# Projection stage of a hybrid streaming trunk: transposes traced one group later, two raw weight buffers, history copies on ScalarE

## The chip, the cores and the metric

The kernel runs on one core of one Trainium2 chip. The metric is the time of one execution on the device in microseconds (us). Of several timed executions the median is taken; a profile describes one further execution, with a time of its own. In the profile PE is TensorE (PEld is its weight load), DVE is VectorE, ACT is ScalarE, POOL is GpSimd, and SP is SyncE, whose queue issues nearly all DMAs.

## The reference

One layer of a streaming encoder with 2048 prompt tokens and 8 x 16 sample tokens, model width 1024, all in float32. Cut to what matters:

```
h = rmsnorm(x, norm1_g) * (1 + sc1) + sh1
proj = h @ w_in                              # 1024 -> q,k,v,gate | beta,a | q,k,v of group B
qkv  = silu(causal depthwise conv, width 4, of proj[q,k,v])     # group A: gated DeltaNet
q, k = l2norm(q) * DK**-0.5, l2norm(k)
o_a  = rmsnorm(chunked delta rule(q, k, v, beta, g)) * silu(gate)
qb, kb = rmsnorm(proj[qB]), rmsnorm(proj[kB])                   # group B: band attention
o_b  = softmax(qb @ kb^T * DH**-0.5 + bias over 9 chunks of 64) @ vb
x = x + gate1 * (concat(o_a, o_b) @ w_out)
x = x + gate2 * (relu(rmsnorm(x) * (1 + sc2) + sh2) @ w_up) ** 2 @ w_down
```

The states are outputs too: the last three rows ahead of the convolution, the delta-rule state, and the last keys and values of group B.

## The kernel before

**Precision and weights.** Each matrix product is made of three passes with operands split into a high and a low part (`hi` x `hi`, `hi` x `lo`, `lo` x `hi`). A weight tile of 512 KB comes to the chip in `weights` (lines 166 to 185): SP loads it into a `raw` buffer (L174, `bufs=self.nraw`), ACT casts it into the high half of a `w` buffer (L175, four buffers), and the low half is either a subtraction on POOL (L82, reading `raw` and the high half), or, once it has been stored, a second load from DRAM (L178). Which one it is depends on the block: `w_in` is subtracted and stored (L183) in the first block of phase 1 and loaded after that; `w_out`, `w_up` and `w_down` are subtracted in block 0 of phase 2, subtracted and stored in block 1, and loaded from block 2 on. So a `raw` buffer is free after the cast, or, where POOL subtracts, after the subtraction. It serves both phases: `run` sets `nraw` once.

**Phase 1** goes over six blocks of two or three tiles of 128 tokens. `proj_a` makes group A's projections: for each of four heads a group of 24 matmuls each for k, q and v (`psq`, L519 to L521, one weight tile, 384 columns), then on the way out of PSUM: two history copies of three columns (L527 before, L529 after), the copy to `pre` (L528, ACT), the convolution (one ACT operation, three DVE operations with `y`), tanh (ACT), and the last product into `kq` or `vT` (DVE). A step registered with `later` runs when `tick` has been called as often as its lag says; `tick` comes once for each group. That step, `qkv_out`, transposes the result on PE (`ptq`, L554), and copies or squares it. `proj_b` makes group B's projections; its keys go through `k_out`, which transposes them (`ptk`, L1011). The delta rule of the block before (lane 0 and 1 of the generators) is put between these groups as filling.

**Phase 2** goes over five blocks of two, four, four, four and three tiles: `out_proj`, then `ffn` with 64 weight tiles per block (32 of `w_up`, 32 of `w_down`); block 0 has two tiles, hence 256 columns per matmul of `w_up` and the shortest time for a weight tile. The attention of the next block's tiles fills in (L1250 to L1292).

**Order.** The Python order sets priorities; a scheduler then fixes each engine's order at build time by its own estimates, so an edit in one place moves rows on every engine. On the chip each engine takes its rows strictly in that order, SP's queue too.

Of the kernel before, what the change touches and what calls it, by code (L numbers as in the profile page):

```python
# [8 lines left out]
F32 = mybir.dt.float32  # L9
F32R = mybir.dt.float32r  # L10
# [4 lines left out]
P = 128  # L15
# [9 lines left out]
DH = 64  # L25
# [16 lines left out]
def bcast(ap, axis, n):  # L42
    dims = [list(x) for x in ap.ap]
    dims.insert(axis, [0, n])
    return bass.AP(tensor=ap.tensor, offset=ap.offset, ap=dims)
# [6 lines left out]
class Trunk:  # L52
# [415 lines left out]
    def proj_a(self, tiles, hT, nxt=()):  # L468

        nc = self.nc  # L470
        n = len(tiles)
        T = n * P
        smp = SMP in tiles
        Tp = T - (P if smp else 0)
        blk = {}
        blk["kq"] = []
        ssq = self.bp.tile([P, self.nt, AH], F32, tag="ssq", name="ssq", bufs=2)
        ssk = self.bp.tile([P, self.nt, AH], F32, tag="ssk", name="ssk", bufs=2)
        ba = self.bp.tile([P, self.nt, 8], F32, tag="ba", name="ba", bufs=2)

        def gates(half):

            xs = [] if half else [self.normed(None, t) for t in nxt]
            m = 256 + 8 * half
            ws = self.wslices("w_in", 0, GA0 + 256 * half, m, KT, 4)
            for j, tl in enumerate(tiles):
                tmps = self.load_a(nxt[j], xs[j], 0, 1) if j < len(xs) else None
                ps = self.gp.tile([P, 512], F32, tag="g", name="psg")
                for k in range(KT):
                    wh, wl = ws[k]  # L490
                    self.mm3(ps[:, 0:m], hT[:, k, 0, j * P:(j + 1) * P], hT[:, k, 1, j * P:(j + 1) * P], wh, wl,
                             k == 0, k == KT - 1)
                th = self.cp.tile([P, 256], F32, tag="th", name="th", bufs=1)
                sg = self.cp.tile([P, 256], F32, tag="sgw", name="sgw", bufs=2)
                self.act(th, ps[:, 0:256], AF.Tanh, scale=0.5)
                self.stt(sg, th, 1.0, ps[:, 0:256], ALU.add, ALU.mult)
                if half:
                    nc.scalar.copy(ba[:, j], ps[:, 256:264])
                sv = sg.rearrange("p (h d) -> p h d", d=P)
                self.tt(sv, sv, bcast(self.gdng, 1, 2), ALU.mult, eng=nc.gpsimd)  # L500
                nc.sync.dma_start(self.s_sg[tl][:, half * 256:(half + 1) * 256], sg)
                self.tick(24 * 256)
                if tmps:
                    self.load_b(j, tmps)
            for j in range(len(tiles), len(xs)):
                self.load_b(j, self.load_a(nxt[j], xs[j], 0, 1))

        gates(1)
        for h in range(AH):
            kq = self.bp.tile([P, 2, self.nt * P], F32, tag="kq", name="kq", bufs=8)  # L510
            blk["kq"].append(kq)
            for sec in (1, 0, 2):
                c = sec * 4 + h
                ws = self.wslices("w_in", 0, c * P, P, KT, KT)
                ps = self.gp.tile([P, 512], F32, tag="g", name="psq")
                for k in range(KT):
                    wh, wl = ws[k]
                    mm = nc.tensor.matmul
                    mm(ps[:, 0:T], wh, hT[:, k, 0, 0:T], start=(k == 0), stop=False)  # L519
                    mm(ps[:, 0:T], wh, hT[:, k, 1, 0:T], start=False, stop=False)  # L520
                    mm(ps[:, 0:T], wl, hT[:, k, 0, 0:T], start=False, stop=(k == KT - 1))  # L521
                self.tick(24 * T)
                pre = self.cp.tile([P, 3 + self.nt * P], F32, tag="pre", name="pre", bufs=2)
                dst = kq[:, 1 - sec] if sec < 2 else self.cp.tile([P, self.nt * P], F32, tag="vT", name="vT", bufs=2)
                y = self.cp.tile([P, self.nt * P], F32, tag="y", name="y", bufs=2)
                if Tp:
                    nc.vector.tensor_copy(pre[:, 0:3], self.hist[:, c])  # L527
                    nc.scalar.copy(pre[:, 3:3 + Tp], ps[:, 0:Tp])  # L528
                    nc.vector.tensor_copy(self.hist[:, c], pre[:, Tp:Tp + 3])  # L529
                    self.conv(y[:, 0:Tp], pre, c, Tp)  # L530
                if smp:
                    pres = self.cp.tile([P, NB, 3 + SL], F32, tag="pres", name="pres", bufs=2)
                    nc.vector.tensor_copy(pres[:, :, 0:3], self.hists[:, c].rearrange("p (b w) -> p b w", w=3))
                    nc.scalar.copy(pres[:, :, 3:], ps[:, Tp:T].rearrange("p (b s) -> p b s", s=SL))
                    nc.vector.tensor_copy(self.hists[:, c].rearrange("p (b w) -> p b w", w=3), pres[:, :, SL:SL + 3])
                    self.conv(y[:, Tp:T].rearrange("p (b s) -> p b s", s=SL), pres, c, P, sub=True)
                th = self.cp.tile([P, self.nt * P], F32, tag="cth", name="cth", bufs=2)
                self.act(th[:, 0:T], y[:, 0:T], AF.Tanh)
                self.stt(dst[:, 0:T], th[:, 0:T], 1.0, y[:, 0:T], ALU.add, ALU.mult)
                self.later(lambda c=c, dst=dst: self.qkv_out(c, dst, tiles, ssq, ssk))  # L540
                if self.bi:
                    self.mod_step()
        self.flush()
        gates(0)
        blk.update(ssq=ssq, ssk=ssk, ba=ba)
        return blk
# [417 lines left out]
    def proj_b_tile(self, sec, half, tl, hT, j, ws):  # L964
        nc = self.nc
        H = BH // 2
        cs = slice(half * 256, (half + 1) * 256)
        hs = slice(half * H, (half + 1) * H)
        ps = self.gp.tile([P, 512], F32, tag="g", name="psb")[:, 0:256]
# [25 lines left out]
        if tl >= 12:  # L995
            nc.sync.dma_start(
                self.o[nm + "band_prompt"][0, 0, (tl - 12) * P:(tl - 11) * P].rearrange("s h d -> s (h d)")[:, cs], raw)
        st = self.qp.tile([P, H, 2, DH], F32R, tag="stk", name="stk", bufs=3)
        self.split(st[:, :, 0], st[:, :, 1], rv)
        if sec == 2:  # L1000
            nc.sync.dma_start(self.s_kv[hs, :, tl, 1].rearrange("h p d -> p h d"), st.bitcast(F32).rearrange("p h a d -> p h (a d)"))
            return
        self.later(lambda: self.k_out(st, hs, tl), 2)

    def k_out(self, st, hs, tl):
        nc = self.nc
# [541 lines left out]
                self.ffn(tiles, self.hT, x1)  # L1548

    def run(self):  # L1550
        self.nraw, self.nw = 3, 4
        self.deferred, self.lanes, self.pending, self.fill_rate, self.fill_acc = [], ([], [], []), [0, 0, 0], 0.0, 0.0
        self.front, self.solved, self.spent = 0, 0, 0
        self.constants()
        self.phase1()
        self.phase2()
# [35 lines left out]
```

## Time and profile before

| what | value |
|---|---|
| median of 3 runs | 3242.33 us (3240.86 to 3249.45) |
| profiled execution, own time | 3235.24 us |
| its span, first to last instruction | 3233.5 us |
| TensorE clock granted, mean | 0.977 |
| PE busy | 3071.4 us, 95% |
| DVE, ACT, POOL busy | 59%, 46%, 22% |
| HBM traffic over the span | 226 GB/s |

Busy shares are means over stages with different limits, and matmul ends are modelled. So the table says that PE is the engine to follow, and that about 160 us of the span are left in which it stands still; where they lie is a question for the view of stretches.

### The profile page before, as it was taken

Reading aid. Unit: us, or ns where it says so; the run is one execution under the profiler, and the core shown is the slowest. Engines: PE = TensorE matmul, PEld = TensorE weight load, DVE = VectorE, ACT = ScalarE, POOL = GpSimd, SP = SyncE. Lnnn points to the kernel's source line nnn. Section 1 sums busy time; section 2 is a strip of 40 time slices with the busy share of each in tenths; the row PEclk is TensorE's granted clock in tenths of the full one; section 3 lists DMA queues with packets and bytes.
Section 4 is the critical chain, followed back from the end, with each engine's and each line's share of the span. In section 5 each row is a group of like instructions: output and inputs, shape, how many; then the busy total and the mean of one; then the engine's idle time right before and its main releaser. Section 6 shows DMA issues by size and latency. Waiting matters only on the chain.

```text
span 3233.5 us, 53068 instructions
## 1 busy us (share of the span) xinstructions
PE 3071.4 (95%) x19577; PEld 2713.0 (84%) x19577; DVE 1903.2 (59%) x4526; ACT 1478.5 (46%) x2707; POOL 701.2 (22%) x561
## 2 busy tenths in 40 slices
PE   7899999999999979988999999999999999998998
PEld 6798988899989968878888889888888887787997
DVE  5985777777868676888446567235455443243223
ACT  3554544556656555554424444344434443333332
POOL 4641312121222347653343320000000000000000
PEclk9999999999989999998999999999999999998999
DMA  9789896878888765565565666665676667677875
GB/s 298 225 264 283 269 288 207 266 236 245 282 292 262 223 201 167 160 222 174 170 200 188 204 214 228 195 195 186 204 246 191 209 230 230 222 239 224 258 246 195
DMA packets 624507, 730.71 MB, mean 226 GB/s; under 512 B 59040, under 2 KB 483088, under 8 KB 622200
## 3 DMA queue, kind: packets, MB, share of 16 engines
q1 hardware_dynamic: 618488, 695.87, 68.0%
q0 software_dynamic: 5760, 31.46, 3.0%
q8 instruction: 154, 2.52, 0.3%
q14 instruction: 105, 0.86, 0.1%
HBM read 614.57 MB, written 115.52 MB: 226 GB/s over the span
## 4 chain that ended last, share of the span: by engine, by line
PE 71%; DVE 12%; DMA 9%; issue 3%; ACT 2%; SPq 1%; POOL 1%; POOLq 0%; DVEq 0%; ACTq 0%
PE psd L164 7%; PE psd L162 7%; PE psu L1480 7%; PE psu L1481 7%; PE psd L163 7%; PE psu L1482 7%; PE pv L1285 2%; PE psq L521 2%; PE psq L520 2%; PE psq L519 2%; PE psb L162 2%; PE psb L164 2%; PE psb L163 2%; PE psS L1267 2%; PE pso L162 2%
## 5 line engine op out<-in xcount | busy, mean ns | idle before, releaser
L175 ACT CAST w<-raw 128x1024 fp32r<-128x1024 f32 (+1 forms) x528 | 552.7, 1048 | 349.2 <-PE psd L164 163.2
L82 POOL TENSOR_TENSOR w<-raw,w 128x1024 fp32r<-128x1024 f32 (+1 forms) x172 | 418.3, 2443 | 365.8 <-ACT w L175 327.5
L1480 PE MATMUL psu<-hT,w 128*128 128x512 f32 (+2 forms) x1304 | 468.6, 361 | 7.1 <-ACT hT L104 6.2
L1481 PE MATMUL psu<-hT,w 128*128 128x512 f32 (+2 forms) x1304 | 467.2, 359 | 1.2 <-DVE hT L82 1.2
L1482 PE MATMUL psu<-hT,w 128*128 128x512 f32 (+2 forms) x1304 | 465.7, 357 | 0.0
L164 PE MATMUL psd<-w,u 128*128 128x512 f32 x1088 | 431.4, 398 | 9.1 <-DVE u L82 9.1
L162 PE MATMUL psd<-w,u 128*128 128x512 f32 x1088 | 432.5, 398 | 7.9 <-DVE y L82 4.1
L163 PE MATMUL psd<-w,u 128*128 128x512 f32 x1088 | 427.6, 393 | 0.0
L82 DVE TENSOR_TENSOR r<-r 128x512 f32<-128x512 f32 (+2 forms) x160 | 178.8, 1117 | 399.7 <-ACT u L92 399.4
L82 DVE TENSOR_TENSOR y<-y,psd 128x512 f32<-128x512 f32 x238 | 162.2, 684 | 242.0 <-PE psd L164 241.4
L1480 PEld LDWEIGHTS psu<-hT,w 128*128 128x128 f32 x1304 | 246.6, 190 | 39.8 <-ACT hT L104 7.4
L1481 PEld LDWEIGHTS psu<-hT,w 128*128 128x128 f32 x1304 | 246.8, 189 | 33.2 <-DVE hT L82 2.3
L1482 PEld LDWEIGHTS psu<-hT,w 128*128 128x128 f32 x1304 | 246.6, 189 | 32.5 <-issue 0.2
L92 ACT ACTIVATE r<-psu 128x512 f32<-128x512 f32 (+2 forms) x160 | 85.5, 534 | 408.7 <-PE psu L1482 349.6
L164 PEld LDWEIGHTS psd<-w,u 128*128 128x128 f32 x1088 | 204.9, 189 | 56.7 <-DVE u L82 10.4
L162 PEld LDWEIGHTS psd<-w,u 128*128 128x128 f32 x1088 | 205.3, 189 | 53.5 <-DVE y L82 6.7
L163 PEld LDWEIGHTS psd<-w,u 128*128 128x128 f32 x1088 | 205.6, 189 | 45.4 <-issue 1.0
L162 PE MATMUL psb<-w,hT 128*128 128x256 f32 x816 | 236.3, 290 | 0.7 <-ACT qraw L976 0.7
L164 PE MATMUL psb<-w,hT 128*128 128x256 f32 x816 | 234.1, 288 | 0.5 <-DVE hT L82 0.5
L163 PE MATMUL psb<-w,hT 128*128 128x256 f32 x816 | 233.4, 287 | 0.0
L520 PE MATMUL psq<-hT,w 128*128 128x384 f32 (+1 forms) x576 | 194.1, 337 | 0.0
L521 PE MATMUL psq<-hT,w 128*128 128x384 f32 (+1 forms) x576 | 193.9, 337 | 0.0
(318 smaller groups left out, 6603.0 us busy)
## 6 DMA issues: line engine op xcount, KB each, us to landing
raw<-in_w_up_dram SPq DMA_DIRECT2D x160, 512.0 KB
raw<-in_w_down_dram SPq DMA_DIRECT2D x160, 512.0 KB
raw<-in_w_in_dram SPq DMA_DIRECT2D x156, 512.0 KB
w<-s_w_in SPq DMA_DIRECT2D x130, 512.0 KB
w<-s_w_up SPq DMA_DIRECT2D x96, 512.0 KB
w<-s_w_down SPq DMA_DIRECT2D x96, 512.0 KB
raw<-in_w_out_dram SPq DMA_DIRECT2D x40, 512.0 KB
x<-in_x_prompt_dram SPq DMA_DIRECT2D x38, 512.0 KB
```

The costliest lines, as they stand in the source:

```text
L82: (eng or self.nc.vector).tensor_tensor(out, in0, in1, op)
L92: self.nc.scalar.activation(out, in_, func, **kw)
L162: mm(out, lh, rh, start=first, stop=False)
L163: mm(out, lh, rl, start=False, stop=False)
L164: mm(out, ll, rh, start=False, stop=last)
L175: nc.scalar.copy(w[:, 0, 0:n], r)
L519: mm(ps[:, 0:T], wh, hT[:, k, 0, 0:T], start=(k == 0), stop=False)
L520: mm(ps[:, 0:T], wh, hT[:, k, 1, 0:T], start=False, stop=False)
L521: mm(ps[:, 0:T], wl, hT[:, k, 0, 0:T], start=False, stop=(k == KT - 1))
L1480: mm(ps[:, c0:c1], wh, h2[:, k, 0, c0:c1], start=(k == 0), stop=False)
L1481: mm(ps[:, c0:c1], wh, h2[:, k, 1, c0:c1], start=False, stop=False)
L1482: mm(ps[:, c0:c1], wl, h2[:, k, 0, c0:c1], start=False, stop=(k == KT - 1))
```

## The change

Five edits. (1) `qkv_out` is registered with lag 2 instead of 1, and `k_out` with lag 3 instead of 2. (2) `vT` gets three buffers instead of two, `stk` four instead of three. (3) Both history copies of a group go from DVE to ACT. (4) The second of them reads the last three columns from PSUM instead of from `pre`. (5) `nraw` is 2 instead of 3, for the whole kernel.

```
-                dst = kq[:, 1 - sec] if sec < 2 else self.cp.tile([P, self.nt * P], F32, tag="vT", name="vT", bufs=2)
+                dst = kq[:, 1 - sec] if sec < 2 else self.cp.tile([P, self.nt * P], F32, tag="vT", name="vT", bufs=3)
...
-                    nc.vector.tensor_copy(pre[:, 0:3], self.hist[:, c])
+                    nc.scalar.copy(pre[:, 0:3], self.hist[:, c])
                     nc.scalar.copy(pre[:, 3:3 + Tp], ps[:, 0:Tp])
-                    nc.vector.tensor_copy(self.hist[:, c], pre[:, Tp:Tp + 3])
+                    nc.scalar.copy(self.hist[:, c], ps[:, Tp - 3:Tp])
...
-                self.later(lambda c=c, dst=dst: self.qkv_out(c, dst, tiles, ssq, ssk))
+                self.later(lambda c=c, dst=dst: self.qkv_out(c, dst, tiles, ssq, ssk), 2)
...
-        st = self.qp.tile([P, H, 2, DH], F32R, tag="stk", name="stk", bufs=3)
+        st = self.qp.tile([P, H, 2, DH], F32R, tag="stk", name="stk", bufs=4)
...
-        self.later(lambda: self.k_out(st, hs, tl), 2)
+        self.later(lambda: self.k_out(st, hs, tl), 3)
...
-        self.nraw, self.nw = 3, 4
+        self.nraw, self.nw = 2, 4
```

Three places in the order that the scheduler makes of it. The first is PE in block 0 of phase 1, where the transposes of the first `vT` (head 0) stand. Before, they stand in the group `psq_961`:

```order
L519 MATMUL psq_961<-hT1_98,w_955 128x384
L520 MATMUL psq_961<-hT1_98,w_955 128x384
L521 MATMUL psq_961<-hT1_98,w_955 128x384
L554 MATMUL ptq_803<-ident_67,vT_751 128x128 x3
L519 MATMUL psq_961<-hT1_98,w_955 128x384
```

Changed, the same transposes stand at the end of the group `psq_829` (the numbers of buffers differ between the two programs):

```order
L519 MATMUL psq_829<-hT1_98,w_823 128x384
L520 MATMUL psq_829<-hT1_98,w_823 128x384
L521 MATMUL psq_829<-hT1_98,w_823 128x384
L554 MATMUL ptq_854<-ident_67,vT_744 128x128 x3
L519 MATMUL psq_889<-hT1_98,w_883 128x384
```

`vT_751` is made from the third group, `psq_718`; before, three whole groups (`psq_778`, `psq_838`, `psq_901`) and a third of the next lie between. Changed, its group is `psq_706`, and two whole groups (`psq_771`, `psq_829`) lie between. Traced one group later, the transposes stand one group nearer in this block. For most of the block's twelve chunks the distance is now two groups and a few rows; before it lies between two and three and a half.

The second place is DVE in the same block, at the first group's convolution. Before:

```order
L529 COPY hist<-pre 128x3
L535 COPY hists<-pres 128x24
L79 SCALAR_TENSOR_TENSOR y<-pre,cw,y 128x256
L79 SCALAR_TENSOR_TENSOR y<-pres,cw,y 128x128
L79 SCALAR_TENSOR_TENSOR y<-pre,cw,y 128x256
L79 SCALAR_TENSOR_TENSOR y<-pres,cw,y 128x128
L79 SCALAR_TENSOR_TENSOR y<-pre,cw,y 128x256
L79 SCALAR_TENSOR_TENSOR y<-pres,cw,y 128x128
L527 COPY pre<-hist 128x3
L533 COPY pres<-hists 128x8x3
```

Changed, on ACT, two groups later in the block:

```order
L528 COPY pre<-psq 128x256
L529 COPY hist<-psq 128x3
L534 COPY pres<-psq 128x8x16
L557 COPY kvw<-ptq 128x384
L92 ACTIVATE y<-pre,cw 128x256
L92 ACTIVATE y<-pres,cw 128x128
L527 COPY pre<-hist 128x3
```

L527 and L529 have left DVE's row of work for ACT's; the copies of the sample rows (L533, L535) stay on DVE.

The third place is SP's queue in block 0 of phase 2, inside `ffn`, with the loads of `raw` and the stores of finished attention heads (`s_ob<-of`). Before:

```order
L174 DMA raw_16053<-in_w_up_dram 128x8x128
L1292 DMA s_ob<-of_16241 64x128
L174 DMA raw_16089<-in_w_down_dram 128x2x512
L174 DMA raw_16094<-in_w_down_dram 128x2x512
L174 DMA raw_16195<-in_w_down_dram 128x2x512
L174 DMA raw_16200<-in_w_down_dram 128x2x512
L174 DMA raw_16270<-in_w_up_dram 128x8x128
```

Changed:

```order
L1292 DMA s_ob<-of_16241 64x128
L174 DMA raw_15975<-in_w_up_dram 128x8x128
L1233 DMA bias_16572<-s_bias 128x640
L174 DMA raw_16053<-in_w_up_dram 128x8x128
L1292 DMA s_ob<-of_16312 64x128
L174 DMA raw_16089<-in_w_down_dram 128x2x512
L174 DMA raw_16094<-in_w_down_dram 128x2x512
L1292 DMA s_ob<-of_16415 64x128
```

The same head's store (`of_16241`) now stands two weight loads earlier, and two more stores come where before were only loads: relative to the attention, the weight stream has moved back. Counted over PE's order, 129 attention matmuls (L1250, L1267, L1275, L1285) are left between this block's last `psd` and the next block's first `psu`; before, 151 are.

## Rows read from the trace of the kernel before

**Rows 1.** Stretches: us, PE, PEld, DVE, ACT, POOL busy; PE clock, DMA share, GB/s.
```profile
46.00:150.00 104.00, 89.94 (x545) 86.63 (x546) 86.27 (x204) 54.42 (x119) 54.22 (x31) 0.93 0.78 248
150.00:225.00 75.00, 67.11 (x524) 65.59 (x524) 61.12 (x140) 36.13 (x77) 40.32 (x28) 0.95 0.78 245
225.00:1160.00 935.00, 895.03 (x7199) 830.10 (x7198) 678.54 (x2121) 507.71 (x1055) 220.54 (x223) 0.97 0.84 263
1160.00:1560.00 400.00, 348.35 (x2293) 314.48 (x2292) 322.42 (x562) 213.43 (x400) 202.65 (x113) 0.94 0.55 171
1560.00:3233.50 1673.50, 1641.35 (x8818) 1398.18 (x8816) 732.88 (x1440) 654.10 (x1042) 165.11 (x130) 0.99 0.67 214
```

**Rows 2.** Waits of PE from 66 to 160 us: total, times, longest.
```profile
PE ptq L554 <- DVE kq L79: 7.2, 4, 3.4
PE ptq L554 <- DVE vT L79: 3.2, 2, 2.8
PE ptk L1011 <- DVE ss L89: 2.6, 1, 2.6
```

**Rows 3.** The window behind the wait of ptk, columns as in the first group.
```profile
160.00:163.40 3.40, 3.40 (x19) 3.40 (x18) 2.42 (x7) 1.83 (x4) 2.70 (x4) 0.50 0.98 346
```

**Rows 4.** Timeline of DVE in block 0: start, duration, instruction.
```profile
83.70 2.32 DVE L527 COPY pre<-hist 128x3 f32<-128x3 f32 x1
```

**Rows 5.** Timeline of POOL in the same microseconds.
```profile
83.47 2.52 POOL L82 TENSOR_TENSOR w<-raw,w 128x1024 fp32r<-128x1024 f32 x1 [1.35 <-ACT w L175]
```

**Rows 6.** Groups of DVE instructions from 46 to 150 us: busy us, mean ns.
```profile
L527 DVE COPY pre<-hist 128x3 f32<-128x3 f32 x14 | 8.2, 587 | 0.0
L529 DVE COPY hist<-pre 128x3 f32<-128x3 f32 x12 | 3.9, 323 | 8.2 <-ACT pre L528 8.2
```

**Rows 7.** Line 527 over the span: durations in ns, minimum, median, maximum.
```profile
L527 DVE COPY pre<-hist x72: 105/161/2353, 47.2 to 881.1; 128x3 f32<-128x3 f32 x72
```

**Rows 8.** Timeline of ACT: a copy of eight columns from PSUM.
```profile
75.25 0.17 ACT L498 COPY ba<-psg 128x8 f32<-128x8 f32 x1 [0.51 <-DVE sgw L79]
```

**Rows 9.** Tile psq from 66 to 83.5 us: first and last start.
```profile
L520 PE MATMUL psq<-hT,w x33: 338/339/339, 65.8 to 83.3; 128*128 128x384 f32 x33
```

**Rows 10.** Tile raw from 1187 to 1433 us: durations, first and last start.
```profile
L175 ACT CAST w<-raw x62: 1031/1046/1068, 1194.0 to 1429.8; 128x1024 fp32r<-128x1024 f32 x62
L82 POOL TENSOR_TENSOR w<-raw,w x62: 2363/2412/2790, 1195.2 to 1430.9; 128x1024 fp32r<-128x1024 f32 x62
```

**Rows 11.** Waits of SP's queue from 1187 to 1433 us: total, times, longest.
```profile
SPq L174 <- POOL w L82: 90.2, 38, 5.6
SPq L1292 <- DVE of L82: 43.0, 16, 5.0
```

**Rows 12.** Timeline of SP's queue, two short stretches of block 0 of phase 2.
```profile
1249.94 1.46 SPq L174 DMA_DIRECT2D raw<-in_w_down_dram  x1
...
1259.57 0.37 SPq L174 DMA_DIRECT2D raw<-in_w_down_dram  x1
...
1279.64 5.74 SPq L174 DMA_DIRECT2D raw<-in_w_down_dram  x3
1287.55 0.37 SPq L174 DMA_DIRECT2D raw<-in_w_up_dram  x1
```

**Rows 13.** Timeline of ACT there: the cast of the load issued at 1249.94.
```profile
1255.99 1.05 ACT L175 CAST w<-raw 128x1024 fp32r<-128x1024 f32 x1 [2.07 <-DMA raw<-in_w_down_dram]
```

**Rows 14.** Line 1285 from 1187 to 1433 us: PE busy, PEld busy, clock, DMA.
```profile
1187.00:1433.00 246.00, 16.34 (x97) 13.69 (x97) 0.98 0.56 167
```

**Rows 15.** Tile raw from 66 to 225 us: loads; what casts and subtractions waited for.
```profile
L174 SPq DMA_DIRECT2D raw<-in_w_in_dram x28: 383/424/1905, 69.4 to 224.6; - x28
...
  DMA raw<-in_w_in_dram: 11.6, 6
```

**Rows 16.** Tile raw from 3000 to 3200 us: the casts, and their only wait.
```profile
L175 ACT CAST w<-raw x48: 1038/1044/1054, 2999.1 to 3195.5; 128x1024 fp32r<-128x1024 f32 x48
...
  PE psd L164: 70.1, 24
```

## The prediction

> **What bounds the kernel now.** I read the stretches first. PE is busy for 1641 of the last 1673.5 us, so nothing in the rest of phase 2 can give much. It stands still for 14 us and 8 us in the two stretches of phase 1's block 0, 40 us in the other blocks of phase 1, and 52 us in block 0 of phase 2 [rows 1]. The change has to act in these 114 us, or open new gaps where there are none.
>
> Then the waits of PE in block 0 of phase 1: the transposes `ptq` wait 10.4 us for the last DVE product of a chunk, and `ptk` 2.6 us [rows 2]. Behind such a wait comes a window of 3.4 us at a granted clock of 0.50, that is 1.2 instead of 2.4 GHz [rows 3]: 1.7 us lost. These are the stalls that the two lags are about.
>
> Why DVE is late there is seen in the two timelines: a copy of three columns takes 2.32 us and ends at 86.02, when POOL's subtraction that began at 83.47 ends at 85.99 [rows 4, 5]. DVE's usual copy of this size takes 0.16 us [rows 7]. In block 0 POOL subtracts for every weight tile, about 2.4 us for each [rows 10], against 4.4 us of PE for a group (32 intervals, eight to a group, in 17.5 us [rows 9]). DVE is 83% busy there, from 46 to 150 us [rows 1].
>
> Last, the raw buffers. In the `ffn` of phase 2's block 0 the casts follow one another at (1429.8 - 1194.0) / 61 = 3.87 us [rows 10], and SP waits 38 times, 90.2 us together, for POOL to give a raw buffer back [rows 11]. So there three buffers are already the limit that SP meets first. At the end of the kernel it is otherwise: 48 casts in 200 us, whose idle time before them is all for PE to free `w`, none for a load [rows 16].
>
> **The change part by part.**
>
> *Two raw buffers, phase 2, block 0.* A raw buffer is held from the issue of its load to the end of the subtraction. A load issued at 1249.94 is cast at 1255.99, and its buffer takes the next load at 1259.57: 9.63 us. One issued at 1279.64 is replaced at 1287.55: 7.91 us [rows 12, 13]. With two buffers a tile comes every half cycle: 3.96 us in the fast case, 4.82 us in the slow one, against 3.87 us now. Over 62 tiles that is +5.5 us or +58.8 us. I weight the fast one two to one, since with two loads in flight instead of three a load has more of the DMA engines: 8.48 us, 4.24 us per tile, 62 x 0.37 = **+23** us. What waits behind: SP's queue is strictly in order, and the stores and loads of the attention (L1292, which already wait 43.0 us for DVE [rows 11]) stand between the raw loads; they are late with them.
>
> *What is moved by it.* In the new order 22 fewer attention matmuls are left after this block's last `psd`. They now lie inside the stretch, where PE waits for weights anyway. At 0.17 us each (16.34 us for 97 [rows 14]) this gives back **-4** us.
>
> *Two raw buffers elsewhere.* In block 0 of phase 1 loads follow one another every 5.75 us (27 intervals from 69.4 to 224.6), and six casts or so waited for their landing, 11.6 us [rows 15]. With two buffers that may be as much again (+11.6), or nothing, as four `w` buffers stand between cast and PE. Most other casts had their data, so I take a quarter: **+3** us. In the later blocks, where the low half is loaded and POOL is out of the cycle, I take nothing: in the last stretch casts are 4.2 us apart, and only PE holds them up [rows 16]. If that cover went, each tile would lie open by what half a cycle exceeds 4.2 us; even a cycle of 8.4 us exceeds it by nothing.
>
> *History copies to ACT.* DVE loses 26 copies in the stretch from 46 to 150 us. They cost it 8.2 + 3.9 = 12.1 us [rows 6], but the long ones are long because POOL holds them up, and then POOL holds up the next DVE instruction instead. At the usual 0.16 us [rows 7] the gain is 26 x 0.16 = **-4** us; the upper bound of the gain is 12.1 us. The Trainium skill, "SBUF — State Buffer", sections on the two separate sides and on who interferes with whom, says that DVE and GpSimd share a port pair held by one of them for a whole instruction, and that ACT never waits for it. The rows on the blocked copy agree. By this rule alone, each copy moved is free of the lock and the sum would take all 12.1 us; I don't, since a blocked queue only passes the block on. On ACT a small copy costs 0.17 us [rows 8]. 144 of them are 24.5 us over phase 1, where ACT is about half idle [rows 1], so nothing; in block 0 they stand in the convolution's chain, and without that cover would cost 24 x 0.17 = +4.
>
> *Lag of qkv_out, third vT buffer.* The order shows that the transposes of block 0 come nearer to their group, not farther: two groups instead of three and a third, about one group of 4.4 us [rows 9]. What the wait measures is DVE's backlog. If DVE works no faster than above, PE waits as long as before, only at another row. I take **0**; bounds are -10.4 us, all of it gone [rows 2], and +4.4 us, a group less in hand.
>
> *Lag of k_out, fourth stk buffer.* The wait of 2.6 us [rows 2] and the half-clock window behind it, 1.7 us [rows 3], go: **-4** us. Nothing is the other bound. Its store goes through SP later by a tile, and is read only by the attention much later.
>
> *Sum.* +23 - 4 + 3 - 4 + 0 - 4 = **+14** us on the profiled execution's own 3235.24 us (span 3233.5 and 1.7 around it), 3249. The median of the runs shown, 3242.33, is 7.1 us above that execution, so on the median **3256**.
>
> **The rivals.** Differences within 0.3% (9.7 us, so 3232.6 to 3252.1) are about what a measurement of this kernel can't tell from no change.
>
> *Two buffers are enough.* If the cycle falls to 7.7 us, two intervals of 3.87, the +23 vanishes, and with it the -4 of moved attention. For it: the fast cycle of 7.91 lies only 0.2 us above [rows 12]. Against it: a second cycle in the same stretch takes 9.63, and SP waits for POOL already with three [rows 11]. Then 0 to +3 - 4 - 4, about -6: 3236. The Trainium skill, "Trainium Kernel Development and Optimization", section "Best Practices", advises double-buffering to overlap DMA with compute. By that rule, two buffers do it and this rival holds; no run here shows two raw buffers yet.
>
> *Block 0 comes untied: faster.* One mechanism: the copies ahead of the convolution no longer sit in DVE's queue behind POOL's lock, so ACT starts the convolution at once, and the chunks are ready in two groups, 8.8 us. Then all waits of PE in [rows 2] go, 13.0 us, and a half-clock window of 1.7 us [rows 3]: -15. It decides if the cycle above is short as well. For it: L529 waited 8.2 us for ACT [rows 6], a knot between both engines that the change removes. Against it: POOL's lock stays, 2.4 us for every group. Time: 3242 - 15 = 3227.
>
> *Slow cycles everywhere.* If ACT and POOL keep the cycle at 9.63 us, the stretch costs 58.8 us, block 0 of phase 1 11.6, and the nearer transposes 4.4: with -4 for the attention +71, 3313. Against it: that load took 6.05 us from issue to cast with three in flight [rows 12, 13], which two would shorten.
>
> **How the numbers follow.** The forecast (weight-bound `ffn` in block 0 of phase 2, little gain in phase 1) gets 0.45; two buffers enough 0.27; block 0 untied 0.18; slow cycles 0.10. The likeliest case alone runs from 3243 to 3280: cycles of 8.1 to 9.0 us (+11 to +39 in place of +23), with some of phase 1's bounds. The range for 8 in 10 reaches down to the untied case and up to a cycle of 9.2 us (+45) with phase 1's unfavourable bounds: 3224 to 3290. Of the forecast 0.05 ends within 0.3%, and of two buffers enough 0.01 below it, so slower has 0.50, no difference 0.31, faster 0.19.
>
> **What would show it.** In the changed kernel's trace: from 1187 us on for about 270 us, casts 4.2 to 4.3 us apart, SP's wait for POOL's subtraction up by more than half, and PE's idle time there up by about 20 us, put down to `w`, to casts or to POOL. Late stretches (3000 to 3200) unchanged, their casts waiting for PE. In block 0 of phase 1 PE's waits for DVE of about the same total, with no L527 and L529 on DVE and each about 0.17 us on ACT; `ptk` with no wait. The prediction is wrong if casts in that `ffn` are still 3.9 us apart, or if the sum of waits on `ptq` in block 0 falls below 4 us.

## The result, and the profile after

The changed kernel takes 3268.57 us (median of 4 runs), the kernel before in the same comparison 3241.60 us (4 runs): ratio 1.0078, 95% interval 1.0062 to 1.0094, so it is slower, by about 25 us (the two medians differ by 27.0). The ratios of this text are of undisturbed executions; one execution of e6 below, 5958.20 us long, is left out of its ratio. The profiled execution took 3269.49 us, its span is 3267.8 us, 34.3 us more than the span of the trace before.

The view of stretches of the changed kernel, for the stretches of [rows 1] (the last runs to the end of the span); columns as there:

```profile
46.00:150.00 104.00, 81.64 (x458) 77.44 (x459) 79.38 (x161) 50.38 (x133) 44.03 (x25) 0.89 0.65 207
150.00:225.00 75.00, 66.09 (x498) 63.62 (x497) 54.61 (x103) 30.61 (x62) 52.78 (x33) 0.94 0.76 232
225.00:1160.00 935.00, 898.32 (x7208) 835.02 (x7207) 679.58 (x2033) 524.12 (x1189) 215.25 (x221) 0.97 0.85 263
1160.00:1560.00 400.00, 342.19 (x2240) 308.52 (x2240) 291.50 (x535) 202.45 (x374) 197.47 (x108) 0.94 0.55 170
1560.00:3267.80 1707.80, 1665.76 (x8976) 1420.39 (x8976) 753.62 (x1493) 676.95 (x1082) 176.75 (x137) 0.99 0.67 214
```

Two places changed. In the first 104 us PE runs 458 matmuls where it ran 545, and 26 more are missing by 225 us. In the stretch around phase 2's block 0 it runs 2240 for 2293. What is left over is done in the last stretch, 158 matmuls more at nearly the same pace (8976 in 1707.8 us, before 8818 in 1673.5).

Fixed stretches cut through work that has moved, so for the rest of the text I cut every trace at the same four events: the first `psq` matmul of phase 1's block 0, the first `psq` of its block 1, the first `pso` of phase 2, and the first `psu` of phase 2's block 1. That makes four pieces: I is block 0 of phase 1, II the rest of phase 1, III block 0 of phase 2 with the `out_proj` of the next, IV the remainder. Lengths in us, worked out from the starts of those matmuls (the experiments e1 to e12 are below):

| kernel | ahead of I | I | II | III | IV |
|---|---|---|---|---|---|
| before | 56.5 | 168.4 | 902.3 | 401.4 | 1704.9 |
| before, second trace (e9) | 56.8 | 170.0 | 907.9 | 402.8 | 1708.2 |
| changed | 56.8 | 184.3 | 897.5 | 423.0 | 1706.3 |
| e1 two raw buffers alone | 57.1 | 173.2 | 899.0 | 426.3 | 1711.5 |
| e10 two raw, phase 2 only | 59.3 | 168.8 | 901.0 | 423.8 | 1716.9 |
| e11 two raw, phase 1 only | 59.7 | 172.5 | 899.6 | 397.2 | 1710.6 |
| e2 all but the raw buffers | 56.4 | 168.4 | 902.4 | 394.8 | 1706.0 |
| e3 history copies alone | 59.0 | 170.8 | 909.9 | 391.4 | 1711.3 |
| e6 lag of `qkv_out` alone | 58.7 | 170.6 | 904.3 | 396.4 | 1707.0 |
| e8 lag of `k_out` alone | 58.9 | 167.8 | 916.3 | 395.1 | 1712.2 |
| e5 two raw + lag of `qkv_out` | 56.5 | 178.3 | 905.5 | 412.6 | 1713.3 |
| e7 two raw + history copies | 56.9 | 180.2 | 898.3 | 412.7 | 1714.4 |
| e12 changed, `vT` and `stk` as before | 57.8 | 183.1 | 891.6 | 425.1 | 1710.5 |
| e4 changed, third raw in phase 2 | 56.4 | 181.6 | 893.4 | 413.9 | 1702.7 |

The two traces of the same kernel before differ by 12.1 us, 5.6 of it in II: single traces can't be read finer than that there. I differs by 1.6 and III by 1.4.

**Phase 2, block 0.** The `ffn` (first `psu` to the last `psd` of line 162) takes 276.0 us in place of 250.7. The view of the tile `raw` inside it, from 1209 to 1483 us: the casts and subtractions, and what these engines waited for ahead of them.

```profile
L175 ACT CAST w<-raw x62: 1032/1048/1054, 1216.7 to 1480.6; 128x1024 fp32r<-128x1024 f32 x62
L82 POOL TENSOR_TENSOR w<-raw,w x62: 2346/2400/2757, 1217.9 to 1481.7; 128x1024 fp32r<-128x1024 f32 x62
...
  DMA raw<-in_w_up_dram: 49.7, 24
  DMA raw<-in_w_down_dram: 25.2, 15
```

Casts follow one another at (1480.6 - 1216.7) / 61 = 4.33 us, before at 3.87 [rows 10]. Both engines now wait 74.9 us for loads to land, 71.1 of it ACT ahead of its casts, where ACT waited 10.4 before. The cycle itself is seen in the timeline of SP, ACT and POOL:

```profile
1295.14 4.85 POOL L82 TENSOR_TENSOR w<-raw,w 128x1024 fp32r<-128x1024 f32 x2 [3.09 <-PE psu L1482]
1297.54 2.84 SPq L174 DMA_DIRECT2D raw<-in_w_down_dram  x2
1302.67 2.19 ACT L175 CAST w<-raw 128x1024 fp32r<-128x1024 f32 x2
1303.80 4.93 POOL L82 TENSOR_TENSOR w<-raw,w 128x1024 fp32r<-128x1024 f32 x2 [3.81 <-DMA raw<-in_w_down_dram]
1306.21 2.91 SPq L174 DMA_DIRECT2D raw<-in_w_up_dram  x2
```

A buffer that POOL gave back at 1297.54, with the first of the two subtractions in the first row, is loaded, cast at 1302.67, subtracted from 1303.80, and loaded again at 1306.21: 8.67 us for two tiles. From issue to cast it is 5.1 us of that, and POOL stands idle 3.81 us until the cast is done. Over the whole stretch (worked out from the starts of SP's loads) a buffer takes its next load after 8.69 us in the mean, 7.28 to 12.40; before, with three buffers, after 11.56 us, 7.91 to 16.59. SP's two rows of waits from 1209 to 1483 us answer to [rows 11]:

```profile
SPq L174 <- POOL w L82: 107.0, 38, 7.6
SPq L1292 <- DVE of L82: 45.2, 19, 5.6
```

**Phase 1, block 0.** PE's waits from 66 to 160 us, to be held against [rows 2]:

```profile
PE ptq L554 <- DVE hists L535: 6.5, 3, 2.8
PE psq L519 <- ACT w L175: 5.6, 2, 4.7
PE ptq L554 <- DVE kq L79: 4.3, 4, 1.4
PE psd L616 <- DVE g L82: 3.4, 1, 3.4
PE psq L521 <- POOL w L82: 1.4, 1, 1.4
```

The transposes wait 10.8 us, as before. New are 7.0 us for the cast or subtraction of a weight, and 3.4 us of the delta rule's filling. The block goes on to 241 us here; from 56 to 242 us three rows more stand among PE's waits:

```profile
PE ptk L1011 <- DVE stk L82: 3.4, 3, 1.8
PE psb L163 <- POOL w L82: 3.2, 3, 2.0
PE psb L162 <- ACT w L175: 2.1, 1, 2.1
```

So in the whole block PE waits 12.3 us for a weight (in the trace before, none), and ACT's casts wait 28.5 us for loads to land (11.6 [rows 15]). All traces here divide this way: with two raw buffers in phase 1 PE's waits for a weight in I are about 6 to 12 us, with three there are none. The granted clock in I is 0.92, before 0.95. What sets the pace is seen in a timeline of ACT, POOL and DVE, one group out of six that repeat like this from 112 to 150 us:

```profile
138.12 1.07 ACT L175 CAST w<-raw 128x1024 fp32r<-128x1024 f32 x1
139.27 2.45 POOL L82 TENSOR_TENSOR w<-raw,w 128x1024 fp32r<-128x1024 f32 x1 [3.70 <-ACT w L175]
139.38 2.63 DVE L79 SCALAR_TENSOR_TENSOR y<-pre,cw,y 128x256 f32<-128x256 f32 x1
141.93 0.34 DVE L79 SCALAR_TENSOR_TENSOR y<-pres,cw,y 128x128 f32<-128x128 f32 x1
142.09 0.19 ACT L527 COPY pre<-hist 128x3 f32<-128x3 f32 x1 [2.90 <-DVE y L79]
142.30 0.52 ACT L92 ACTIVATE cth<-y 128x384 f32<-128x384 f32 x1
142.73 0.35 ACT L528 COPY pre<-psq 128x256 f32<-128x256 f32 x1
143.98 0.42 ACT L92 ACTIVATE y<-pres,cw 128x128 f32<-128x128 f32 x1
144.27 1.06 ACT L175 CAST w<-raw 128x1024 fp32r<-128x1024 f32 x1
```

It is a ring. The cast starts POOL's subtraction; a DVE product that takes 0.48 us elsewhere is held up to 2.63 by it; ACT waits 2.90 us for that product, ahead of the tanh (`cth`), the copies out of PSUM and the next convolution; and the next cast stands in ACT's queue behind all of these. Each group takes 144.27 - 138.12 = 6.15 us, where PE needs 4.4 [rows 9]. Before, ACT's order varies from group to group, and from 66 to 160 us casts come 2.0 to 8.5 us apart. That the ring alone makes the block longer is not shown (e7 below).

The history copies have left DVE, as lines by form from 46 to 150 us show (compare [rows 6]). The last two rows are the convolution's long product on DVE, before and changed:

```profile
L527 ACT COPY pre<-hist 128x3 f32<-128x3 f32 x13 | 2.4, 193 | 34.8 <-DVE y L79 33.5 <-PE ptm L316 1.2
L529 ACT COPY hist<-psq 128x3 f32<-128x3 f32 x12 | 2.0, 165 | 0.0
L79 DVE SCALAR_TENSOR_TENSOR y<-pre,cw,y 128x256 f32<-128x256 f32 x36 | 21.4, 594 | 1.1 <-ACT y L92 0.9
L79 DVE SCALAR_TENSOR_TENSOR y<-pre,cw,y 128x256 f32<-128x256 f32 x33 | 35.4, 1074 | 1.8 <-ACT y L92 1.8
```

DVE is rid of 12.1 us of copies and spends 14.0 us more on these products, three fewer of them: POOL's block has passed to the next instruction.

And in the late stretch, 3000 to 3200 us, as in [rows 16], the casts are still 4.2 us apart ((3198.6 - 2999.0) / 48) and wait chiefly for PE, but now 11.7 us for loads too:

```profile
L175 ACT CAST w<-raw x49: 1037/1047/1056, 2999.0 to 3198.6; 128x1024 fp32r<-128x1024 f32 x49
...
  PE psd L164: 53.3, 19
  DMA raw<-in_w_up_dram: 9.3, 3
  DMA raw<-in_w_down_dram: 2.4, 5
```

### The profile page after: what moved, and what is told of

Its sections match the earlier page's. It is cut to its first block, busy times and chain, and to the rows that moved or that the text cites. A ratio compares the mean times of both kernels' runs of the same rounds, so it can differ in the third digit from the quotient of the medians.

```text
span 3267.8 us, 52908 instructions
## 1 busy us (share of the span) xinstructions
PE 3082.2 (94%) x19577; PEld 2721.8 (83%) x19577; DVE 1880.9 (58%) x4382; ACT 1495.7 (46%) x2851; POOL 702.1 (21%) x561
## 4 chain that ended last, share of the span: by engine, by line
PE 55%; DMA 7%; DVE 5%; issue 3%; ACT 2%; POOL 2%; SPq 0%; POOLq 0%; ACTq 0%; DVEq 0%
PE psu L1480 7%; PE psu L1482 7%; PE psu L1481 7%; PE psd L162 7%; PE psd L163 7%; PE psd L164 7%; DMA raw<-in_w_up_dram 2%; POOL w L82 1%; PE pv L1285 1%; PE psP L1275 1%; PE psS L1267 1%; PE pso L162 1%; PE pso L164 1%; PE pso L163 1%; DMA raw<-in_w_down_dram 1%
## 5 line engine op out<-in xcount | busy, mean ns | idle before, releaser
L82 DVE TENSOR_TENSOR r<-r 128x512 f32<-128x512 f32 (+2 forms) x160 | 159.1, 994 | 411.4 <-ACT u L92 410.9
L1480 PEld LDWEIGHTS psu<-hT,w 128*128 128x128 f32 x1304 | 249.9, 192 | 41.6 <-ACT hT L104 6.5
L1482 PEld LDWEIGHTS psu<-hT,w 128*128 128x128 f32 x1304 | 248.5, 191 | 42.4 <-POOL w L82 9.4
L1481 PEld LDWEIGHTS psu<-hT,w 128*128 128x128 f32 x1304 | 249.1, 191 | 35.3 <-DVE hT L82 2.3
L162 PE MATMUL psb<-w,hT 128*128 128x256 f32 x816 | 238.5, 295 | 4.8 <-ACT w L175 3.5
L163 PE MATMUL psb<-w,hT 128*128 128x256 f32 x816 | 237.3, 292 | 3.5 <-POOL w L82 3.2
L164 PE MATMUL psb<-w,hT 128*128 128x256 f32 x816 | 237.2, 292 | 0.1
```

The lines of the kernel that those rows point to most:

```text
L82: (eng or self.nc.vector).tensor_tensor(out, in0, in1, op)
L162: mm(out, lh, rh, start=first, stop=False)
L163: mm(out, lh, rl, start=False, stop=False)
L164: mm(out, ll, rh, start=False, stop=last)
L1480: mm(ps[:, c0:c1], wh, h2[:, k, 0, c0:c1], start=(k == 0), stop=False)
L1481: mm(ps[:, c0:c1], wh, h2[:, k, 1, c0:c1], start=False, stop=False)
```

## The experiments

Theory A after the result: two raw buffers are nearly the whole loss, and what they cost is paid in block 0 of phase 2, with a part in block 0 of phase 1. The rival, theory B: the transposes and history copies, as they now stand, cost time in phase 1 by themselves. Later expectations name theories of their own under the same letters.

**e1: two raw buffers alone.** The kernel before with

```
-        self.nraw, self.nw = 3, 4
+        self.nraw, self.nw = 2, 4
```

> The kernel before with two raw buffers instead of three and nothing else. Theory A (the raw buffers cause nearly all of the loss, in both places): 24 to 38 us slower than before; the ffn of phase 2's block 0 longer by 20 to 30 us, the first block of phase 1 up to its first psb by 10 to 20 us. Theory B (raw buffers cost only in that ffn; the loss in block 0 of phase 1 comes from where the transposes and copies stand): 10 to 18 us slower, block 0 of phase 1 longer by less than 4 us.

Measured: ratio 1.0089, 1.0073 to 1.0106, that is +29 us. Piece III takes 426.3 us, as changed; I only 173.2. The total is theory A's. Block 0 of phase 1 up to its first `psb` is 4 to 6 us longer than in the two traces before, between the two theories and nearer to B.

**e2: all but the raw buffers.** The kernel before with both lags and the history copies on ACT; three raw buffers, and `vT` and `stk` as before.

```
+                    nc.scalar.copy(pre[:, 0:3], self.hist[:, c])
+                    nc.scalar.copy(self.hist[:, c], ps[:, Tp - 3:Tp])
+                self.later(lambda c=c, dst=dst: self.qkv_out(c, dst, tiles, ssq, ssk), 2)
+        self.later(lambda: self.k_out(st, hs, tl), 3)
```

> The rest of the change on three raw buffers: both lags one longer, history copies on ACT; vT stays at two buffers and stk at three, since deeper ones don't fit beside three raw buffers. Theory A: 8 us faster to 4 us slower, block 0 of phase 1 up to its first psb within 5 us of before. Theory B: 8 to 20 us slower, all of it in block 0 of phase 1.

Measured: ratio 0.9955, 0.9938 to 0.9973: about 15 us faster than before, more than theory A gave, and at 3231.55 us the fastest kernel of this study. I is untouched at 168.4 us; III takes 394.8 in place of 401.4 and 402.8. Theory B falls as a cause by itself: without the two buffers these edits cost nothing. Why they gain is not shown: of 5.5 us between the two profiled spans, III has all, and none of the edits lies there.

**e3: history copies alone.**

```
+                    nc.scalar.copy(pre[:, 0:3], self.hist[:, c])
+                    nc.scalar.copy(self.hist[:, c], ps[:, Tp - 3:Tp])
```

> The history copies on ACT alone, all else as before. My prediction's term: 4 us faster, by DVE's 26 small copies in block 0. Rival by the port rule: about 12 us faster. Rival that the copies lengthen the convolution's chain on ACT: 4 us slower. The order of PE's transposes in block 0 is the same as before, so this run shows the copies without the move.

Measured: ratio 0.9990, 0.9979 to 1.0001: a gain of 3 us, not told apart from nothing.

**e4: the changed kernel with a third raw buffer in phase 2.** Every third weight tile of phase 2 uses a buffer of its own.

```
+        if self.xr is not None and self.nld % (self.nraw + 1) >= self.nraw:
+            r = self.xr.tile([P, 1056], F32, tag="rawx", name="raw", bufs=1)[:, 0:n]
```

> The changed kernel with a third raw buffer in phase 2 alone (every third load there takes a buffer of its own pool). Theory A: casts in the ffn of block 0 of phase 2 again about 3.9 us apart, that stretch 20 to 28 us shorter than in the changed kernel, and the whole 15 to 25 us shorter, so 2 to 14 us slower than before. Rival (the stretch is slow from DVE and ACT as the new order places them, not from raw buffers): no more than 6 us shorter than the changed kernel.

Measured: ratio 1.0038, 1.0022 to 1.0055. About half of the loss is gone; the `ffn` of block 0 takes 254.6 us, its casts are 3.9 us apart, as theory A says. But 12 us remain, and against e2 it is 25. In the traces I is still 181.6 us, II 893.4, and III 413.9 against 402 before, 9 us of that between the first `pso` and the first `psu`. Why that third buffer does not restore all of it is open; what differs from e2 is two raw buffers in phase 1, the deeper `vT` and `stk`, a buffer in a pool of its own, and the order that comes of these.

**e5: two raw buffers and the lag of `qkv_out`.**

```
+                self.later(lambda c=c, dst=dst: self.qkv_out(c, dst, tiles, ssq, ssk), 2)
+        self.nraw, self.nw = 2, 4
```

> The kernel before with two raw buffers and the lag of qkv_out at 2; vT and stk as deep as before, history copies on DVE, lag of k_out as before. Looked at first is the stretch from the first psq matmul of phase 1's block 0 to the first of block 1: 168.4 us before, 184.3 changed, 173.2 with two raw buffers alone, 168.4 with all but the raw buffers. Theory A (lockstep): the loss of block 0 needs two raw buffers and the later transposes together, because only then ACT's row stands, group after group, as cast, tanh, copy out of psq, first convolution, cast; the cast starts POOL's subtraction, which holds up DVE's last product of the convolution, on which the next tanh waits. Then casts in the second half of the block are 6.0 to 6.2 us apart, the stretch takes 181 to 186 us, PE's waits for ptq come at nearly every group, and the median lies 24 to 36 us above before. Theory B (history copies): the loss needs the copy of the history on ACT, which writes pre and so waits for DVE ahead of the next tanh; then the stretch stays at 171 to 176 us as with two raw buffers alone.

Measured: ratio 1.0073, 1.0048 to 1.0097, +24 us, the lower edge of theory A's range. The casts in the timeline of ACT, in the second half of the block:

```profile
120.20 1.05 ACT L175 CAST w<-raw 128x1024 fp32r<-128x1024 f32 x1
126.58 1.07 ACT L175 CAST w<-raw 128x1024 fp32r<-128x1024 f32 x1
132.67 1.06 ACT L175 CAST w<-raw 128x1024 fp32r<-128x1024 f32 x1
138.75 1.05 ACT L175 CAST w<-raw 128x1024 fp32r<-128x1024 f32 x1
```

They are 6.1 to 6.4 us apart with the history still on DVE, so the ring needs no history copy. Piece I takes 178.3 us, less than the 181 to 186 expected.

**e6: the lag of `qkv_out` alone,** with three raw buffers.

```
+                self.later(lambda c=c, dst=dst: self.qkv_out(c, dst, tiles, ssq, ssk), 2)
```

> The kernel before with the lag of qkv_out at 2 and nothing else; three raw buffers. Theory A (lockstep needs two raw buffers): block 0 of phase 1 takes 167 to 171 us as before. If the 0.45% that all but the raw buffers won came from this lag, the median lies 10 to 16 us below before; if it came from the history copies or k_out, it lies within 5 us of before. On record the lag was put at 0 with bounds -10.4 and +4.4 us.

Measured: ratio 0.9980, 0.9965 to 0.9996: about 6 us faster, between the two cases of the expectation. Piece I takes 170.6 us, like the second trace of before, so the lag won nothing there.

**e7: two raw buffers and the history copies.**

```
+                    nc.scalar.copy(pre[:, 0:3], self.hist[:, c])
+                    nc.scalar.copy(self.hist[:, c], ps[:, Tp - 3:Tp])
+        self.nraw, self.nw = 2, 4
```

> The kernel before with two raw buffers and both history copies on ACT; lags and depths as before. Theory A (lockstep of two raw buffers and the lag): block 0 of phase 1 takes 171 to 176 us, as with two raw buffers alone, casts there are unevenly spaced, and the median is that of two raw buffers alone, 24 to 32 us above before. Theory B (history copies close the ring): block 0 takes 181 to 186 us and the median is 34 to 44 us above before.

Measured: ratio 1.0058, 1.0036 to 1.0079, +19 us, below what either theory gave. Piece I takes 180.2 us, which was theory B's side, but the casts come 4.7 to 7.6 us apart:

```profile
99.43 1.06 ACT L175 CAST w<-raw 128x1024 fp32r<-128x1024 f32 x1
104.78 1.06 ACT L175 CAST w<-raw 128x1024 fp32r<-128x1024 f32 x1
112.36 1.06 ACT L175 CAST w<-raw 128x1024 fp32r<-128x1024 f32 x1
117.04 1.05 ACT L175 CAST w<-raw 128x1024 fp32r<-128x1024 f32 x1 [2.10 <-DMA raw<-in_w_in_dram]
```

So with two raw buffers either edit lengthens block 0, with or without an even ring, and neither theory had that. And a longer block 0 does not carry through: e7 has the longest piece I of the experiments made on the kernel before, and the smallest loss of those with two raw buffers in phase 2.

**e8: the lag of `k_out` alone.**

```
+        self.later(lambda: self.k_out(st, hs, tl), 3)
```

> The kernel before with the lag of k_out at 3 and nothing else (stk stays at three buffers). By the term on record: PE's first wait for ptk in block 0, 2.6 us, and the half-clock window behind it are gone, the median 2 to 6 us below before. Rival: in the runs with both lags ptk still waits 1 to 2 us once or twice, so the wait only moves, and the median is within 3 us of before.

Measured: ratio 0.9983, 0.9968 to 0.9999: about 5 us faster, the size on record. But PE's waits from 66 to 165 us still hold this row:

```profile
PE ptk L1011 <- DVE ss L89: 2.4, 1, 2.4
```

The wait that the lag was to remove is there, 2.4 us for 2.6 [rows 2] and for 2.4 in the second trace of before (e9). PE's first 900 matmuls, up to 172 us, stand in the same order as before, those that wait among them. The gain is not that term. Where it comes from the trace can't tell, as its execution is the slowest of e8's twelve (3252.14 us, the median is 3239.98): II is 916.3 us in it, but III only 395.1, where no key of phase 1 is transposed and only the scheduler's order has changed.

**e9: the kernel before, once more, for a second trace.**

> The kernel before, unchanged, for a second trace of it. Its ffn of phase 2's block 0 took 250.7 us in the first trace, with casts 3.92 us apart; the four other kernels with three raw buffers took 240 to 243 us there, with 3.76 to 3.81. If this is the spread of single executions, the second trace takes 240 to 246 us there; if the edits of those kernels shortened it, the second trace takes 248 to 253. Block 0 of phase 1, to the first matmul of block 1, should take 167 to 170 us again (168.4).

Measured: one run, 3247.32 us. The `ffn` of block 0 takes 248.5 us, piece I 170.0. The `ffn` is where it was expected if the edits of the others shorten it: so the 240 to 243 us of the other kernels with three raw buffers go with their orders, as far as two traces can tell, and not with the spread of single executions. e11, with three raw buffers there and none of the other edits, fits too: 397.2 us for III.

**e10: two raw buffers in phase 2 alone.** The third buffer gets a tag of its own, and the flag `three` is false in phase 2.

```
+        self.nld, x = self.nld + 1, self.three and self.nld % 3 == 2
+        r = self.wp.tile([P, 1056], F32, tag="rawx" if x else "raw", name="raw", bufs=1 if x else 2)[:, 0:n]
```

> The kernel before with two raw buffers in phase 2 alone (the third is kept, and used in phase 1 only). Theory A (the term on record: a cycle of a raw buffer shared by two instead of three): block 0 of phase 1 as before, 167 to 170 us; in the ffn of phase 2's block 0 casts 4.3 to 4.5 us apart and 20 to 36 us more, a part of it given back in the attention behind it; median 14 to 24 us above before. Theory B (two buffers cost as much in phase 1 and the way into phase 2, as the 13 us suggest that the third buffer in phase 2 won back of the changed kernel's 27): median 8 to 13 us above before.

Measured: ratio 1.0091, 1.0070 to 1.0113, +30 us, above theory A's range and as much as two buffers everywhere (+29). The tile `raw` from 1195 to 1472 us:

```profile
L176 ACT CAST w<-raw x62: 1028/1047/1067, 1201.4 to 1471.1; 128x1024 fp32r<-128x1024 f32 x62
...
  DMA raw<-in_w_up_dram: 46.8, 22
  DMA raw<-in_w_down_dram: 21.5, 14
```

Casts are (1471.1 - 1201.4) / 61 = 4.42 us apart, and ACT waits 68.3 us for loads. Piece III is 21 to 22 us longer than before. IV is 9 to 12 us longer in this trace, for which no cause is shown.

**e11: two raw buffers in phase 1 alone.** The lines of e10, with the flag the other way round.

```
+        self.nw, self.nld, self.three = 4, 0, False
+        self.three = True
```

> The kernel before with two raw buffers in phase 1 alone, three in phase 2. Theory A: block 0 of phase 1 takes 171 to 176 us as with two everywhere, later blocks of phase 1 give some of it back, the ffn of phase 2's block 0 has casts 3.7 to 3.9 us apart; median 0 to 7 us above before (+3 on record, bounds 0 and +11.6). Theory B: median 10 to 18 us above before.

Measured: ratio 0.9997, 0.9983 to 1.0011: nothing, theory A's side. Piece I takes 172.5 us, 2.5 to 4 more than before, and it does not reach the total.

**e12: the changed kernel with `vT` at two and `stk` at three buffers.**

```
-                dst = kq[:, 1 - sec] if sec < 2 else self.cp.tile([P, self.nt * P], F32, tag="vT", name="vT", bufs=3)
-        st = self.qp.tile([P, H, 2, DH], F32R, tag="stk", name="stk", bufs=4)
+                dst = kq[:, 1 - sec] if sec < 2 else self.cp.tile([P, self.nt * P], F32, tag="vT", name="vT", bufs=2)
+        st = self.qp.tile([P, H, 2, DH], F32R, tag="stk", name="stk", bufs=3)
```

> The changed kernel with vT at two and stk at three buffers, as before: both lags, history copies on ACT and two raw buffers remain. All but the raw buffers won 0.45% (about -15 us), two raw buffers alone cost 0.89% (about +29); the changed kernel lies 27 us above before, 13 more than their sum. Theory A (lag, history copies and two raw buffers together close the ring of cast, subtraction, last product and history copy in block 0): casts there 6.1 to 6.4 us apart, the stretch to block 1 takes 181 to 186 us as changed, median 22 to 32 us above before. Theory B (the deeper vT and stk take the rest): the median is 9 to 18 us above before, the sum of the parts.

Measured: ratio 1.0070, 1.0054 to 1.0086, +23 us, and piece I takes 183.1 us with casts 6.1 to 6.5 us apart. That is theory A's side, near its edge: the deeper buffers are not what is missing between the sum of the parts and the whole.

## Why the prediction was right, and where its parts were off

The forecast was the weight-bound `ffn` of phase 2's block 0, with little from phase 1, at 3256 us in a range of 3224 to 3290. That is the case that came, at 3268.57. Its mechanism is shown on the kernel before: two raw buffers in phase 2 alone cost as much as two everywhere (e10, e1), and two in phase 1 alone cost nothing (e11). In the traces at hand casts in that `ffn` are 4.3 to 4.5 us apart in every kernel with two raw buffers there, and 3.75 to 3.9 in every one with three, whatever its order. In the changed kernel it is shown for half: a third buffer in phase 2 wins back 13 us of the 25 (e4). Point by point:

- *Two raw buffers in phase 2, +23.* Right. The cycle was put at 8.48 us for two tiles and is 8.69 in the mean and 2 x 4.33 by the casts; (4.33 - 3.87) x 62 = 28.5 us. Two raw buffers lengthen III by 16 to 30 us, depending on the edits beside them (e5 less e6, e7 less e3, e1 and e10 less before, e12 less e2). The `ffn` became 25.3 us longer than in the first trace of before, 27.5 longer than in the second. The fast end (+5.5) and the slow end (+58.8) did not come. The weight of two to one towards the fast cycle was about 5 us too hopeful. There is luck in its two readings: of the 58 cycles in that stretch, 7.91 is the shortest and 9.63 among the shorter, while the mean is 11.56 us, which is three times 3.87. With two loads at a time the mean from issue to cast fell from 7.2 to 4.6 us (worked out from the starts of SP's loads and ACT's casts), so a cycle near the short end came; that it fell because a load has more of the DMA engines is not shown.
- *How it shows.* Partly wrong. PE's idle time in that stretch rose from 24.9 us (246 less 221.12 busy) to 36.1, by 11 and not 20, while 350 attention matmuls stand in the `ffn` where 308 stood, about 7 us at the prediction's 0.17 each; the granted clock there is 0.96, before 0.98. And SP's wait for POOL rose from 90.2 to 107.0, a fifth and not half. The time stands instead in ACT's wait for landings, 10.4 us before and 71.1 after: with two buffers ACT is done with what has landed before the next load is there. The late stretch is as forecast but for 11.7 us of waits for loads.
- *Attention moved into the stretch, -4.* Mis-sized, and only one of two moves. From the last `psd` to the next `psu` the changed kernel takes 75.8 us, before 90.6: -14.8. Half of that is idle time of PE (8.4 us there, before 15.7). The other half is busy time (67.4 us for 74.9), of which the 22 matmuls at 0.17 us make 3.7; the granted clock there is 0.97, before 0.89, which the term did not count. But from the first `pso` to the first `psu` 11 us were added (71.1 for 60.1), with 77 attention matmuls in place of 89. All of piece III is 20.2 to 21.6 us longer; the prediction's +23 - 4 was 19.
- *Two raw buffers in phase 1, +3.* e11 says 0, within the bounds, and there I is 2.5 to 4 us longer. In the changed kernel the cover by four `w` buffers did not hold: PE waits 12.3 us for weights in I, and I is 14 to 16 us longer. How much of that reaches the total is not shown; II is 5 to 10 us shorter, and two traces of one kernel differ by 5.6 there.
- *History copies, -4.* e3 gives -3, not told apart from 0. The 12.1 us bound, every long copy gained, is excluded by the interval; that POOL's lock moves to the next DVE instruction is seen in the ring, and in the 14.0 us that the convolution's products gained.
- *Lag of `qkv_out`, 0.* e6 gives -6, within the bounds. The waits for `ptq` in block 0 stayed about the same, as argued, and with them piece I. The gain lies elsewhere, and the prediction had no step for it.
- *Lag of `k_out`, -4.* Size right by luck, reason wrong: the wait that was to go is there in e8, and in the changed kernel `ptk` waits 3.4 us, in three goes, where none was expected.
- *The sum, +14.* This is where the forecast came out short, by about 11 us. Measured singly the parts are +29 (e1) and -15 (e2), which is again +14, or 0.44%. That the sums agree is luck: the forecast had +22 and -8 for these parts, each off by 7 us. The whole is 0.78% (e12, nearly the same kernel, 0.70%). Half an interval is 0.17 and 0.18 for the parts, so their sum is uncertain by about 0.25, and the excess of 0.26 to 0.34%, 8 to 11 us, by about 0.30: it is at the edge of what these runs tell. Two places speak for it. The three edits shorten III from 402 to 394.8 us when three raw buffers are there, but with two the raw cycle sets the pace, and III takes 423 to 426 us with or without them (e1, e10, changed, e12). And block 0 of phase 1 takes 182 to 184 us only with all of them (changed, e4, e12). Against it stand e5 and e7, where one of the edits with two raw buffers gives III 412.6 us. Which of the two places holds the excess, if it is there, stays open.

The rival "two buffers are enough" needed casts 3.9 us apart; they are 4.33. "Block 0 untied" needed the waits for `ptq` to go; they are 10.8 us. "Slow cycles everywhere" needed 4.82 us per tile.

On the Trainium skill's advice to double-buffer, "Trainium Kernel Development and Optimization", section "Best Practices": it doesn't hold in this stage, where a tile passes three owners in turn (issue to cast 5.1 us in the cycle shown, cast 1.05, subtraction 2.4) and PE can use one every 3.87 us or less; 8.67 us of cycle are 2.2 times that, so they ask for three. Where PE needs 4.2 us per tile and POOL is out of the cycle, as at the end of the kernel, two are enough (IV is 1706.3 us, before 1704.9 and 1708.2), and the rule agrees.

## What to carry to other kernels

Divide the time for which a buffer is held, from the issue of its load to its last reader, by the pace at which its consumer takes tiles, stage by stage: the quotient, rounded up, is the number of buffers, and the stage with the largest decides. Where the buffers are already the limit, the mean only gives back their number (11.56 / 3.87 = 3 here), so the time must be one without queueing; here the shortest, 7.91 us, gives 2.04, and the run with two buffers 2.2. Measure a bundle of edits part by part: here three of them won 0.45%, by a way that is not shown, and a fourth, which paid for memory that the others didn't need, cost 0.9%. Before a gain is put down to the wait that an edit was aimed at, look whether the wait is gone; with a scheduler between code and chip it may be there still.

## What was not expected of the hardware

A ring over three engines, with none of them fully busy (DVE 32.2, ACT 20.7 and POOL 14.6 of the 38 us from 112 to 150): cast on ACT, subtraction on POOL, a DVE product stretched from 0.48 to 2.63 us beside it, and ACT's queue waiting for that product ahead of its next cast, 6.15 us per turn. Also the spread of one kernel: 17 executions of the kernel before, taken beside e9, lie between 3237.71 and 3259.07 us, and its two traces, with the same order of instructions on every engine, differ by 12.1 us, of which piece II has 5.6. Why the two differ is not shown.
